# Rotary embedding with scaled positions on one core: rows of 16 KB, fp32 stores from SyncE, and a copy inside DRAM ahead of the positions

## The chip, the core and the metric

The kernel runs on one core of a Trainium2 chip. A core has five engines that run their own instruction streams: TensorE (PE in the profile, with PEld for its weight loads), VectorE (DVE), ScalarE (ACT), GpSimd (POOL) and SyncE (SP). SP, ScalarE and POOL also issue DMA transfers, which 16 DMA engines carry out. Each issuer has a queue of its own on each of them. The metric is the device time of one execution in microseconds (us), as a median over runs. The profile shows one execution.

## The reference

Input x has the shape (8, 8, 1024, 64) in fp32. Position and frequency give an angle, and each row of 64 values is turned by it, the first half against the second:

```python
    half = x.shape[-1] // 2
    scaled_positions = positions * scale
    angles = np.outer(scaled_positions, freqs)
    cos = np.cos(angles)
    sin = np.sin(angles)
    ...
    out_first = x_first * cos - x_second * sin
    out_second = x_first * sin + x_second * cos
    return np.concatenate([out_first, out_second], axis=-1).astype(np.float32)
```

Here scale is 0.5, positions run from 0 to 1023, and there are 32 frequencies. Input and output are 16.8 MB each. Sine and cosine depend on position and frequency alone and are the same for all 64 heads.

## The kernel before

The 64 heads are cut into 16 units of four heads (1 MiB of fp32 each). In a unit each of the 128 partitions holds 32 consecutive positions of one head: a row of 2048 values, 8 KB in DRAM (lines 42 to 46). Because 32 partitions make one head, partition p holds the same positions in every unit, and one table of sines and one of cosines (128 x 1024, fp16) serve all of them.

Loads: unit 0 is loaded in fp32 by SP (line 63). The other fifteen are loaded by POOL in seven DMAs of one to three units, cast to fp16 on the way (lines 76 to 81, `GROUPS`). ScalarE's queue brings the positions, four DMAs that each fill 32 partitions with the same 1024 positions (lines 67 to 71), and then the frequencies (line 73).

Setup: TensorE multiplies a row of constants with the frequencies, which spreads them, scaled, over all partitions in PSUM (`cfreq`, line 87). VectorE casts the positions (`posf`, line 90) and forms the angle in turns (`y`, line 95). The helper `reduced` takes off whole turns with the rounding constant `_MAGIC` in two instructions (lines 107 and 109); it runs once for the sine and, after a quarter turn is added (line 115), once for the cosine. ScalarE evaluates `Sin` for both (lines 117 and 119).

Main loop (lines 124 to 138), for each unit: two products of the whole unit, `pc` with the cosine and `ps` with the sine, then a subtraction and an addition over one half each, written into the fp16 tile `OUT`. All four run on VectorE. POOL stores `OUT` with a cast to fp32 (line 138). There are three buffers each for `pc` and `ps` and ten for `OUT`. The inputs have a buffer for every unit, so no load waits for a free one.

Order: a scheduler places the instructions and their waits from what each reads and writes. Each engine runs its own stream in order, and each queue takes its DMAs in the order of issue. POOL's stores therefore stand behind POOL's loads.

Of the kernel before, what the change touches and what calls it, by code (L numbers as in the profile page):

```python
# [1 line left out]

# [1 line left out]

# [4 lines left out]

FP32 = mybir.dt.float32
FP16 = mybir.dt.float16
I32 = mybir.dt.int32
AF = mybir.ActivationFunctionType
ALU = mybir.AluOpType

_MAGIC = 12582912.0
_TWO_PI_DN = float(np.float32(np.uint32(0x40C90FDA).view(np.float32)))


GROUPS = (1, 1, 2, 2, 3, 3, 3)
BUF_O = 10
BUF_P = 3


@with_exitstack
def kernel(
    ctx: ExitStack,
    tc: tile.TileContext,
    x: bass.AP,  # L30
    freqs: bass.AP,
    positions: bass.AP,
    scale: bass.AP,
    out: bass.AP,
):
    nc = tc.nc

    B, Hh, S, D = x.shape
    NBH = B * Hh
    half = D // 2  # L40
    P = nc.NUM_PARTITIONS
    HEADS = 4
    HP = P // HEADS
    K = S // HP
    N = K * D
    NU = NBH // HEADS
    assert S % HP == 0 and D == 2 * half and NBH % HEADS == 0 and sum(GROUPS) == NU - 1

    fscale = float(scale)

    xv = x.rearrange("b h s d -> (b h s d)").rearrange("(u p n) -> p u n", p=P, n=N)
    ov = out.rearrange("b h s d -> (b h s d)").rearrange("(u p n) -> p u n", p=P, n=N)

    consts = ctx.enter_context(tc.tile_pool(name="consts", bufs=1))
    tmp = ctx.enter_context(tc.tile_pool(name="tmp", bufs=1))
    setup_psum = ctx.enter_context(tc.tile_pool(name="setup_psum", bufs=1, space=bass.MemoryType.PSUM))
    xin = ctx.enter_context(tc.tile_pool(name="xin", bufs=1))
    xout = ctx.enter_context(tc.tile_pool(name="xout", bufs=BUF_O))
    prods = ctx.enter_context(tc.tile_pool(name="prods", bufs=BUF_P))


    X0 = xin.tile([P, N], FP32, name="X0")
    nc.sync.dma_start(out=X0, in_=xv[:, 0, :])
    xtiles = {0: X0}

    pos_i64 = consts.tile([P, K], positions.dtype)
    for h in range(HEADS):
        nc.scalar.dma_start(  # L68
            out=pos_i64[h * HP : (h + 1) * HP, :],
            in_=positions.rearrange("(q k) -> q k", k=K),  # L70
        )
    freq_row = consts.tile([1, half], FP32)
    nc.scalar.dma_start(out=freq_row, in_=freqs[None, :])

    u0 = 1
    for g, n in enumerate(GROUPS):
        X = xin.tile([P, n, N], FP16, name=f"X{g + 1}")
        nc.gpsimd.dma_start(out=X, in_=xv[:, u0 : u0 + n, :])  # L78
        for i in range(n):
            xtiles[u0 + i] = X[:, i, :]  # L80
        u0 += n


    coef = consts.tile([1, P], FP32)
    nc.vector.memset(coef, fscale / (2.0 * np.pi))  # L85
    cfreq = setup_psum.tile([P, half], FP32)
    nc.tensor.matmul(out=cfreq, lhsT=coef, rhs=freq_row, start=True, stop=True)  # L87

    posf = consts.tile([P, K], FP32)
    nc.vector.tensor_copy(  # L90
        out=posf,
        in_=pos_i64.bitcast(I32).rearrange("p (k t) -> p k t", t=2)[:, :, 0],
    )
    y = tmp.tile([P, K, half], FP32)
    nc.vector.tensor_tensor(  # L95
        out=y,
        in0=posf.unsqueeze(2).broadcast_to((P, K, half)),
        in1=cfreq.unsqueeze(1).broadcast_to((P, K, half)),
        op=ALU.mult,
    )  # L100

    cosT = consts.tile([P, K, half], FP16)
    sinT = consts.tile([P, K, half], FP16)

    def reduced(src, tag):
        m = tmp.tile([P, K, half], FP32, name="m" + tag)
        nc.vector.tensor_scalar(out=m, in0=src, scalar1=_MAGIC, scalar2=None, op0=ALU.add)  # L107
        rneg = tmp.tile([P, K, half], FP32, name="rneg" + tag)
        nc.vector.scalar_tensor_tensor(  # L109
            out=rneg, in0=m, scalar=_MAGIC, in1=src, op0=ALU.subtract, op1=ALU.subtract  # L110
        )
        return rneg

    yc = tmp.tile([P, K, half], FP32)
    nc.vector.tensor_scalar(out=yc, in0=y, scalar1=0.25, scalar2=None, op0=ALU.add)  # L115
    rc = reduced(yc, "c")
    nc.scalar.activation(out=cosT, in_=rc, func=AF.Sin, bias=0.0, scale=-_TWO_PI_DN)  # L117
    rs = reduced(y, "s")
    nc.scalar.activation(out=sinT, in_=rs, func=AF.Sin, bias=0.0, scale=-_TWO_PI_DN)  # L119
    cos_b = cosT.unsqueeze(2).broadcast_to((P, K, 2, half))  # L120
    sin_b = sinT.unsqueeze(2).broadcast_to((P, K, 2, half))


    for u in range(NU):
        X = xtiles.pop(u).rearrange("p (k h j) -> p k h j", h=2, j=half)
        pc = prods.tile([P, K, 2, half], FP16, tag="pc")
        ps = prods.tile([P, K, 2, half], FP16, tag="ps")
        nc.vector.tensor_tensor(out=pc, in0=X, in1=cos_b, op=ALU.mult)  # L128
        nc.vector.tensor_tensor(out=ps, in0=X, in1=sin_b, op=ALU.mult)  # L129

        OUT = xout.tile([P, K, 2, half], FP16, tag="O")
        nc.vector.tensor_tensor(  # L132
            out=OUT[:, :, 0, :], in0=pc[:, :, 0, :], in1=ps[:, :, 1, :], op=ALU.subtract
        )
        nc.vector.tensor_tensor(  # L135
            out=OUT[:, :, 1, :], in0=ps[:, :, 0, :], in1=pc[:, :, 1, :], op=ALU.add
        )
        nc.gpsimd.dma_start(out=ov[:, u, :], in_=OUT.rearrange("p k h j -> p (k h j)"))  # L138


# [1 line left out]
_INS = ['x', 'freqs', 'positions', 'scale']  # L142
_OUTS = [((8, 8, 1024, 64), 'float32')]

_NUMBERS = {'scale': 0.5}


# [26 lines left out]
```

## Time and profile before

| | |
|---|---|
| median of 10 runs | 85.99 us (85.86 to 86.16) |
| the profiled execution | 86.14 us, its span 84.4 us |
| busy: VectorE / POOL / ScalarE / TensorE | 63.6 / 13.7 / 3.4 / 0.6 us |
| share of the span taken by packets of POOL's DMA queue (16 engines) | 98.9% |
| bytes read from and written to HBM | 16.81 MB and 16.78 MB |
| y, the first work on both positions and frequencies, starts | 9.18 us |
| last VectorE instruction starts / last store is issued | 71.85 / 72.83 us |

The span runs from the first to the last instruction that the profile holds; the device time lies about 1.7 us above it. In rows of groups, "128x2048 f16" is partitions x elements per partition and type, "x15" the count; after the bar come the busy time, the mean of one in ns, and the idle time of the engine before them with what ended it. In the slices a digit is the busy share in tenths. A DMA row names the issuing queue, the size, and the median time from issue to landing. Queue q0 is POOL's, q1 SP's, q10 ScalarE's. The window rows give, for a stretch, each engine's busy time, the clock, the share of the DMA engines' time and the GB/s that they wrote.

### The profile page before, as it was taken

How to read it: one execution, taken by the hardware profiler on the slowest of the kernel's cores; microseconds unless marked ns; L12 is line 12 of the kernel's file. 1: busy time of each engine (PE TensorE's matmuls, PEld its weight loads, DVE VectorE, ACT ScalarE, POOL GpSimd, SP SyncE). 2: the span in 40 equal slices, each digit the busy share in tenths (PEclk: the TensorE clock that was granted, in tenths of full speed). 3: DMA queues.
4: the chain of work that ended last, by engine and by line, in shares of the span. 5: the costliest groups of instructions: out<-in, count | busy, mean ns of one | idle time of the engine just before them, and what ended most of it. 6: DMA issues, size and time to landing. Idle time of an engine off the chain costs nothing.

```text
span 84.4 us, 183 instructions
## 1 busy us (share of the span) xinstructions
PE 0.6 (1%) x2; PEld 0.5 (1%) x2; DVE 63.6 (75%) x72; ACT 3.4 (4%) x3; POOL 13.7 (16%) x27
## 2 busy tenths in 40 slices
PE   0000200000000000000000000000000000000000
PEld 0000200000000000000000000000000000000000
DVE  0000699999999999999999999999999999300000
ACT  0410005400000000000000000000000000000000
POOL 5980000000202202112021020220202202200000
DMA  1899999999999999999999999999999999999970
GB/s 16 338 284 206 216 216 216 216 218 210 216 212 210 218 216 216 216 216 218 165 418 423 435 420 427 420 431 431 431 431 420 435 420 423 431 431 423 435 284 0
DMA packets 4675, 25.73 MB, mean 305 GB/s; under 512 B 578, under 2 KB 578, under 8 KB 2498
## 3 DMA queue, kind: packets, MB, share of 16 engines
q0 software_dynamic: 4336, 24.64, 98.9%
q1 hardware_dynamic: 144, 1.05, 3.3%
q10 hardware_dynamic: 194, 0.03, 0.3%
q14 instruction: 1, 0.01, 0.0%
HBM read 16.81 MB, written 16.78 MB: 398 GB/s over the span
## 4 chain that ended last, share of the span: by engine, by line
DVE 38%; issue 32%; DMA 7%; POOL 6%; ACTq 2%; POOLq 1%; PE 1%
DVE pc L128 12%; DVE ps L129 11%; DMA freq_row<-in_freqs_dram 7%; POOL out_dram L138 6%; DVE OUT L135 5%; DVE OUT L132 5%; ACTq L68 2%; DVE y L95 1%; DVE rnegc L109 1%; DVE yc L115 1%; PE cfreq L87 1%; DVE ms L107 1%; DVE mc L107 1%; POOLq L169 1%; POOLq L138 0%
## 5 line engine op out<-in xcount | busy, mean ns | idle before, releaser
L129 DVE TENSOR_TENSOR ps<-X,sinT 128x2048 f16<-128x2048 f16 (+1 forms) x16 | 20.5, 1282 | 0.0
L128 DVE TENSOR_TENSOR pc<-X,cosT 128x2048 f16<-128x2048 f16 (+1 forms) x16 | 20.4, 1281 | 0.0
L138 POOL DMA_DIRECT2D out_dram<-OUT x16 | 8.6, 538 | 58.6 <-DVE OUT L135 58.6
L132 DVE TENSOR_TENSOR OUT<-pc,ps 128x1024 f16<-128x1024 f16 x16 | 10.9, 682 | 0.0
L135 DVE TENSOR_TENSOR OUT<-ps,pc 128x1024 f16<-128x1024 f16 x16 | 10.9, 681 | 0.0
L90 DVE CAST posf<-pos_i 128x32 f32<-128x32 int32 x1 | 0.2, 181 | 7.1 <-DMA pos_i<-in_positions_dram 7.1
L78 POOL DMA_DIRECT2D X<-in_x_dram x7 | 4.9, 714 | 0.8 <-POOLq L155 0.8
L95 DVE TENSOR_TENSOR y<-posf,cfreq 128x1024 f32<-128x1024 f32 x1 | 1.2, 1222 | 0.9 <-PE cfreq L87 0.9
L119 ACT ACTIVATE sinT<-rnegs 128x1024 f16<-128x1024 f32 x1 | 1.1, 1057 | 9.0 <-DVE rnegs L109 9.0
L119 ACT ACT_TABLE_LOAD x1 | 1.3, 1283 | 3.2 <-issue 3.2
L109 DVE SCALAR_TENSOR_TENSOR rnegc<-mc,yc 128x1024 f32<-128x1024 f32 x1 | 1.2, 1217 | 0.0
L109 DVE SCALAR_TENSOR_TENSOR rnegs<-ms,y 128x1024 f32<-128x1024 f32 x1 | 1.2, 1215 | 0.0
L117 ACT ACTIVATE cosT<-rnegc 128x1024 f16<-128x1024 f32 x1 | 1.1, 1057 | 0.1
L85 DVE MEMSET coef<- 1x128 f32 x1 | 0.2, 165 | 0.8 <-PEq L155 0.8
L115 DVE TENSOR_SCALAR yc<-y 128x1024 f32<-128x1024 f32 x1 | 0.7, 693 | 0.0
L107 DVE TENSOR_SCALAR ms<-y 128x1024 f32<-128x1024 f32 x1 | 0.7, 686 | 0.0
L107 DVE TENSOR_SCALAR mc<-yc 128x1024 f32<-128x1024 f32 x1 | 0.7, 685 | 0.0
L87 PE MATMUL cfreq<-freq_row,coef 1*128 1x32 f32 x2 | 0.6, 392 | 8.5 <-DMA freq_row<-in_freqs_dram 8.5
L87 PEld LDWEIGHTS cfreq<-freq_row,coef 1*128 1x128 f32 x2 | 0.5, 306 | 8.5 <-DVE posf L90 8.5
L155 POOL MEMSET const-float32-0.0<- 128x1 f32 x1 | 0.1, 99 | 0.2 <-issue 0.2
L155 POOL MEMSET const-bfloat16-1.0<- 128x1 bf16 x1 | 0.1, 102 | 0.0
L155 POOL MEMSET const-uint8-127<- 128x1 uint8 x1 | 0.1, 100 | 0.0
(1 smaller groups left out, 0.1 us busy)
## 6 DMA issues: line engine op xcount, KB each, us to landing
out_dram<-OUT POOLq DMA_DIRECT2D x16, 1024.0 KB, 16.6
X<-in_x_dram POOLq DMA_DIRECT2D x3, 1536.0 KB, 30.7
X<-in_x_dram POOLq DMA_DIRECT2D x2, 1024.0 KB, 15.4
X<-in_x_dram SPq DMA_DIRECT2D x1, 1024.0 KB, 5.1
X<-in_x_dram POOLq DMA_DIRECT2D x2, 512.0 KB, 8.0
pos_i<-in_positions_dram ACTq DMA_DIRECT2D x4, 8.0 KB, 5.0
freq_row<-in_freqs_dram ACTq DMA_DIRECT2D x1, 0.1 KB
```

The lines of the kernel that those rows point to most:

```text
L68: nc.scalar.dma_start(out=pos_i64[h * HP : (h + 1) * HP, :], in_=positions.rearrange("(q k) -> q k", k=K),)
L78: nc.gpsimd.dma_start(out=X, in_=xv[:, u0 : u0 + n, :])
L87: nc.tensor.matmul(out=cfreq, lhsT=coef, rhs=freq_row, start=True, stop=True)
L95: nc.vector.tensor_tensor(out=y, in0=posf.unsqueeze(2).broadcast_to((P, K, half)), in1=cfreq.unsqueeze(1).broadcast_to((P, K, half)), op=A ...
L107: nc.vector.tensor_scalar(out=m, in0=src, scalar1=_MAGIC, scalar2=None, op0=ALU.add)
L109: nc.vector.scalar_tensor_tensor(out=rneg, in0=m, scalar=_MAGIC, in1=src, op0=ALU.subtract, op1=ALU.subtract)
L119: nc.scalar.activation(out=sinT, in_=rs, func=AF.Sin, bias=0.0, scale=-_TWO_PI_DN)
L128: nc.vector.tensor_tensor(out=pc, in0=X, in1=cos_b, op=ALU.mult)
L129: nc.vector.tensor_tensor(out=ps, in0=X, in1=sin_b, op=ALU.mult)
L132: nc.vector.tensor_tensor(out=OUT[:, :, 0, :], in0=pc[:, :, 0, :], in1=ps[:, :, 1, :], op=ALU.subtract)
L135: nc.vector.tensor_tensor(out=OUT[:, :, 1, :], in0=ps[:, :, 0, :], in1=pc[:, :, 1, :], op=ALU.add)
L138: nc.gpsimd.dma_start(out=ov[:, u, :], in_=OUT.rearrange("p k h j -> p (k h j)"))
```

## The change

A unit is now eight heads, 2 MiB: each partition holds 64 positions, a row of 4096 values, 16 KB in DRAM. There are 8 units. Unit 0 still comes in fp32 from SP, and ScalarE casts it into an fp16 tile. Units 1 to 7 come from POOL, one DMA each, cast to fp16. The loop takes unit 1 before unit 0. In the loop only `ps` has a tile of its own; the cosine product, the subtraction and the addition are written into the input tile. ScalarE then copies the result to an fp32 tile (four buffers), and SP stores that.

The first DMA on ScalarE's queue is new: it copies 16 rows of 512 bytes from x to out inside DRAM, two to each unit's part of out. The unit stores later write over them. Positions are loaded once, onto 16 partitions, and a matmul with a 0/1 matrix `sel`, which POOL builds, spreads them over 128. The range reduction runs once; the cosine comes from the absolute value of the reduced angle (sign bit masked off) and a bias of a quarter turn. `pin` keeps instructions of an engine in the order in which they are written.

```diff
--- before.py
+++ after.py
@@ -17,10 +17,8 @@
 _MAGIC = 12582912.0
 _TWO_PI_DN = float(np.float32(np.uint32(0x40C90FDA).view(np.float32)))
 
-
-GROUPS = (1, 1, 2, 2, 3, 3, 3)
-BUF_O = 10
-BUF_P = 3
+BUF_O = 4
+BUF_P = 2
 
 
 @with_exitstack
@@ -39,103 +37,118 @@
     NBH = B * Hh
     half = D // 2
     P = nc.NUM_PARTITIONS
-    HEADS = 4
+    HEADS = 8
     HP = P // HEADS
     K = S // HP
     N = K * D
     NU = NBH // HEADS
-    assert S % HP == 0 and D == 2 * half and NBH % HEADS == 0 and sum(GROUPS) == NU - 1
+    assert S % HP == 0 and D == 2 * half and NBH % HEADS == 0
 
     fscale = float(scale)
 
-    xv = x.rearrange("b h s d -> (b h s d)").rearrange("(u p n) -> p u n", p=P, n=N)
-    ov = out.rearrange("b h s d -> (b h s d)").rearrange("(u p n) -> p u n", p=P, n=N)
+    xv = x.rearrange("b h s d -> (b h s d)").rearrange("(u p n) -> u p n", p=P, n=N)
+    ov = out.rearrange("b h s d -> (b h s d)").rearrange("(u p n) -> u p n", p=P, n=N)
 
     consts = ctx.enter_context(tc.tile_pool(name="consts", bufs=1))
     tmp = ctx.enter_context(tc.tile_pool(name="tmp", bufs=1))
-    setup_psum = ctx.enter_context(tc.tile_pool(name="setup_psum", bufs=1, space=bass.MemoryType.PSUM))
+    psum = ctx.enter_context(tc.tile_pool(name="psum", bufs=1, space=bass.MemoryType.PSUM))
     xin = ctx.enter_context(tc.tile_pool(name="xin", bufs=1))
     xout = ctx.enter_context(tc.tile_pool(name="xout", bufs=BUF_O))
     prods = ctx.enter_context(tc.tile_pool(name="prods", bufs=BUF_P))
 
 
-    X0 = xin.tile([P, N], FP32, name="X0")
-    nc.sync.dma_start(out=X0, in_=xv[:, 0, :])
-    xtiles = {0: X0}
+    X0f = xin.tile([P, N], FP32, name="X0f")
+    nc.sync.dma_start(out=X0f, in_=xv[0])
 
-    pos_i64 = consts.tile([P, K], positions.dtype)
-    for h in range(HEADS):
-        nc.scalar.dma_start(
-            out=pos_i64[h * HP : (h + 1) * HP, :],
-            in_=positions.rearrange("(q k) -> q k", k=K),
-        )
+
+    R = 16
+    xr = x.rearrange("b h s d -> (b h s d)").rearrange("(r n) -> r n", r=R)
+    outr = out.rearrange("b h s d -> (b h s d)").rearrange("(r n) -> r n", r=R)
+    nc.scalar.dma_start(out=outr[:, 0:128], in_=xr[:, 0:128])
+
+    pos_i64 = consts.tile([HP, K], positions.dtype)
+    nc.scalar.dma_start(out=pos_i64, in_=positions.rearrange("(q k) -> q k", k=K))
     freq_row = consts.tile([1, half], FP32)
     nc.scalar.dma_start(out=freq_row, in_=freqs[None, :])
 
-    u0 = 1
-    for g, n in enumerate(GROUPS):
-        X = xin.tile([P, n, N], FP16, name=f"X{g + 1}")
-        nc.gpsimd.dma_start(out=X, in_=xv[:, u0 : u0 + n, :])
-        for i in range(n):
-            xtiles[u0 + i] = X[:, i, :]
-        u0 += n
+    X = [xin.tile([P, K, 2, half], FP16, name=f"X{u}") for u in range(NU)]
+
+    def load(u):
+        nc.gpsimd.dma_start(out=X[u].rearrange("p k h j -> p (k h j)"), in_=xv[u])
+
+
+    sel = consts.tile([HP, HEADS, HP], FP32)
+    load(1)
+    nc.gpsimd.memset(sel, 0.0)
+    nc.gpsimd.affine_select(
+        out=sel, in_=sel, compare_op=ALU.not_equal, fill=1.0, base=0,
+        pattern=[[0, HEADS], [-1, HP]], channel_multiplier=1,
+    )
+    for u in range(2, NU):
+        load(u)
+
+    pin = tc.keep_in_program_order
 
 
     coef = consts.tile([1, P], FP32)
-    nc.vector.memset(coef, fscale / (2.0 * np.pi))
-    cfreq = setup_psum.tile([P, half], FP32)
+    pin(nc.vector.memset(coef, fscale / (2.0 * np.pi)))
+    quarter = consts.tile([P, 1], FP32)
+    pin(nc.vector.memset(quarter, np.pi / 2.0))
+    cfreq = psum.tile([P, half], FP32)
     nc.tensor.matmul(out=cfreq, lhsT=coef, rhs=freq_row, start=True, stop=True)
 
+    pos_row = consts.tile([HP, K], FP32)
+    pin(nc.vector.tensor_copy(
+        out=pos_row,
+        in_=pos_i64.bitcast(I32).rearrange("p (k t) -> p k t", t=2)[:, :, 0],
+    ))
+    pos_ps = psum.tile([P, K], FP32)
+    nc.tensor.matmul(
+        out=pos_ps, lhsT=sel.rearrange("q a b -> q (a b)"), rhs=pos_row, start=True, stop=True
+    )
     posf = consts.tile([P, K], FP32)
-    nc.vector.tensor_copy(
-        out=posf,
-        in_=pos_i64.bitcast(I32).rearrange("p (k t) -> p k t", t=2)[:, :, 0],
-    )
+    pin(nc.vector.tensor_copy(out=posf, in_=pos_ps))
+
     y = tmp.tile([P, K, half], FP32)
-    nc.vector.tensor_tensor(
+    pin(nc.vector.tensor_tensor(
         out=y,
         in0=posf.unsqueeze(2).broadcast_to((P, K, half)),
         in1=cfreq.unsqueeze(1).broadcast_to((P, K, half)),
         op=ALU.mult,
-    )
+    ))
+    m = tmp.tile([P, K, half], FP32)
+    pin(nc.vector.tensor_scalar(out=m, in0=y, scalar1=_MAGIC, scalar2=None, op0=ALU.add))
+    r = tmp.tile([P, K, half], FP32)
+    pin(nc.vector.scalar_tensor_tensor(
+        out=r, in0=m, scalar=_MAGIC, in1=y, op0=ALU.subtract, op1=ALU.subtract
+    ))
+    sinT = consts.tile([P, K, half], FP16)
+    pin(nc.scalar.activation(out=sinT, in_=r, func=AF.Sin, bias=0.0, scale=-_TWO_PI_DN))
+    ra = tmp.tile([P, K, half], FP32)
+    pin(nc.vector.tensor_scalar(
+        out=ra.bitcast(I32), in0=r.bitcast(I32), scalar1=0x7FFFFFFF, scalar2=None, op0=ALU.bitwise_and
+    ))
+    cosT = consts.tile([P, K, half], FP16)
+    pin(nc.scalar.activation(out=cosT, in_=ra, func=AF.Sin, bias=quarter, scale=-_TWO_PI_DN))
+    pin(nc.scalar.copy(out=X[0].rearrange("p k h j -> p (k h j)"), in_=X0f))
 
-    cosT = consts.tile([P, K, half], FP16)
-    sinT = consts.tile([P, K, half], FP16)
-
-    def reduced(src, tag):
-        m = tmp.tile([P, K, half], FP32, name="m" + tag)
-        nc.vector.tensor_scalar(out=m, in0=src, scalar1=_MAGIC, scalar2=None, op0=ALU.add)
-        rneg = tmp.tile([P, K, half], FP32, name="rneg" + tag)
-        nc.vector.scalar_tensor_tensor(
-            out=rneg, in0=m, scalar=_MAGIC, in1=src, op0=ALU.subtract, op1=ALU.subtract
-        )
-        return rneg
-
-    yc = tmp.tile([P, K, half], FP32)
-    nc.vector.tensor_scalar(out=yc, in0=y, scalar1=0.25, scalar2=None, op0=ALU.add)
-    rc = reduced(yc, "c")
-    nc.scalar.activation(out=cosT, in_=rc, func=AF.Sin, bias=0.0, scale=-_TWO_PI_DN)
-    rs = reduced(y, "s")
-    nc.scalar.activation(out=sinT, in_=rs, func=AF.Sin, bias=0.0, scale=-_TWO_PI_DN)
     cos_b = cosT.unsqueeze(2).broadcast_to((P, K, 2, half))
     sin_b = sinT.unsqueeze(2).broadcast_to((P, K, 2, half))
 
 
-    for u in range(NU):
-        X = xtiles.pop(u).rearrange("p (k h j) -> p k h j", h=2, j=half)
-        pc = prods.tile([P, K, 2, half], FP16, tag="pc")
+    for u in (1, 0, *range(2, NU)):
         ps = prods.tile([P, K, 2, half], FP16, tag="ps")
-        nc.vector.tensor_tensor(out=pc, in0=X, in1=cos_b, op=ALU.mult)
-        nc.vector.tensor_tensor(out=ps, in0=X, in1=sin_b, op=ALU.mult)
-
-        OUT = xout.tile([P, K, 2, half], FP16, tag="O")
-        nc.vector.tensor_tensor(
-            out=OUT[:, :, 0, :], in0=pc[:, :, 0, :], in1=ps[:, :, 1, :], op=ALU.subtract
-        )
-        nc.vector.tensor_tensor(
-            out=OUT[:, :, 1, :], in0=ps[:, :, 0, :], in1=pc[:, :, 1, :], op=ALU.add
-        )
-        nc.gpsimd.dma_start(out=ov[:, u, :], in_=OUT.rearrange("p k h j -> p (k h j)"))
+        pin(nc.vector.tensor_tensor(out=ps, in0=X[u], in1=sin_b, op=ALU.mult))
+        pin(nc.vector.tensor_tensor(out=X[u], in0=X[u], in1=cos_b, op=ALU.mult))
+        pin(nc.vector.tensor_tensor(
+            out=X[u][:, :, 0, :], in0=X[u][:, :, 0, :], in1=ps[:, :, 1, :], op=ALU.subtract
+        ))
+        pin(nc.vector.tensor_tensor(
+            out=X[u][:, :, 1, :], in0=ps[:, :, 0, :], in1=X[u][:, :, 1, :], op=ALU.add
+        ))
+        OUT = xout.tile([P, N], FP32, tag="O")
+        pin(nc.scalar.copy(out=OUT, in_=X[u].rearrange("p k h j -> p (k h j)")))
+        nc.sync.dma_start(out=ov[u], in_=OUT)
 
 
 # ---- launch: one core; inputs and outputs as the reference has them ----
```

## The prediction

> **What bounds the kernel now.** I read the page first, then windows, then the DMA queues of the first microseconds, then the costliest groups. The page (40 slices; GB/s counts bytes as written):
>
> ```profile
> span 84.4 us, 183 instructions
> ...
> DVE  0000699999999999999999999999999999300000
> ...
> DMA  1899999999999999999999999999999999999970
> GB/s 16 338 284 206 216 216 216 216 218 210 216 212 210 218 216 216 216 216 218 165 418 423 435 420 427 420 431 431 431 431 420 435 420 423 431 431 423 435 284 0
> ```
>
> VectorE ends near 72.5 us, the DMA engines work until about 82. So transfers set the end. Windows (length, each engine's busy time, clock, DMA share, GB/s) show two phases:
>
> ```profile
> 10.00:40.00 30.00, 0.00 (x0) 0.00 (x0) 29.97 (x33) 2.11 (x2) 3.29 (x6) 1.00 1.07 215
> 40.00:42.50 2.50, 0.00 (x0) 0.00 (x0) 2.50 (x4) 0.00 (x0) 0.00 (x0) 1.00 0.97 185
> 44.00:79.00 35.00, 0.00 (x0) 0.00 (x0) 28.50 (x34) 0.00 (x0) 4.80 (x9) 1.00 1.12 427
> ```
>
> Loads come first, because the stores stand behind them in POOL's queue. 215 GB/s written in fp16 is 430 read in fp32; the stores write 427. Either way about 428 GB/s of fp32, and the 33.59 MB that HBM read and wrote (16.81 + 16.78) take 78.5 us at that rate.
>
> The setup is the other chain. Three windows of the DMA queues, 2.50 to 3.95, 3.95 to 4.85 and 4.85 to 5.55 us (packets, MB, share; q1 is SP's X0, q10 ScalarE's positions and frequencies, q0 POOL's):
>
> ```profile
> q10 hardware_dynamic: 48, 0.01, 3.1%
> ...
> q1 hardware_dynamic: 46, 0.38, 102.3%
> ...
> q0 software_dynamic: 25, 0.10, 73.1%
> q1 hardware_dynamic: 23, 0.06, 21.5%
> q10 hardware_dynamic: 53, 0.01, 7.8%
> ```
>
> 48 packets are one position DMA (32 data, 16 completions). The first got in between X0's packets; the second, issued at 1.17 us, moved nothing until X0 ran out, and then went at once, as did q0. What ScalarE issues second waits for all of X0. Critical chain (start, duration) and groups:
>
> ```profile
> 2.58 5.83 DMA freq_row<-in_freqs_dram
> 8.54 0.62 PE cfreq L87 x2
> 9.18 1.23 DVE y L95
> ```
> ```profile
> L129 DVE TENSOR_TENSOR ps<-X,sinT 128x2048 f16<-128x2048 f16 x15 | 18.2, 1215 | 0.0
> L132 DVE TENSOR_TENSOR OUT<-pc,ps 128x1024 f16<-128x1024 f16 x16 | 10.9, 682 | 0.0
> L119 ACT ACTIVATE sinT<-rnegs 128x1024 f16<-128x1024 f32 x1 | 1.1, 1057 | 9.0 <-DVE rnegs L109 9.0
> ...
> X<-in_x_dram SPq DMA_DIRECT2D x1, 1024.0 KB, 5.1
> ```
>
> **What the Trainium skill says.** "VectorE: DVE Perf Modes", The perf-mode tier table: a 16-bit tensor-tensor of 2048 elements takes 1224 ns; the trace has 1215, and in-place operands keep type and stride, so I keep that rate. "DMA: Bandwidth & Descriptors", Queues, rings and completion order: each DMA engine takes turns between queues by packet. The trace agrees once q0 runs, but not from 3.95 to 4.85; the measurement decides. Same page, Latency and other measured facts: copies of 128 x 16 KiB tiles between HBM tensors reach 214 GB/s per direction, 428 together; no run here yet shows mixed traffic, so this is why I assume no loss from it.
>
> **The change part by part.**
>
> *Bytes and stores.* The fp32 bytes stay. A floor: SP's X0 took 5.10 us from issue (0.74) to landing, 2.45 of it for 1.05 MB at 428, so 2.65 us is start, ramp and completion. 0.74 + 2.65 + 78.5 = 81.9 if the engines never idle. The last store now lands at 72.83 + 9.8 = 82.6, leaving 1.8 us to the span's end. Floor: 83.7, against 84.4; the gain is the dip at 40 to 42.5 us and ragged ends.
>
> *Setup, ScalarE's queue.* Three position DMAs go (0.44 us of issue each); a copy inside DRAM comes first, at 0.74. It takes the place of the first position DMA, the one that got in. Positions become second, frequencies third. X0f is twice X0: the q1 packets that ended between 4.9 and 5.5 us end at 7.3 to 8.0 (+2.45). Then positions land at about 8.3. Frequencies need a data and a completion packet, each behind one of q0's (0.33 us now, perhaps double with longer rows): landing about 9.3, against 8.41. The wait holds TensorE, then VectorE's y, and everything after it.
>
> *Positions spread by a matmul.* From frequencies to y took 0.77 us (8.41 to 9.18). A second matmul and a copy out of PSUM come between, unless TensorE does the positions first: 0 to 0.9, I take 0.5. y starts at 10.6. POOL builds the selector after its first load; no row shows its cost, but it has until 8.3 us, and X1's 4.9 us of transfer covers the delay of the later loads. Nothing.
>
> *Tables.* 2048 elements instead of 1024. y and the subtraction 2.29 each (the fp32 form of L129 took 2293 ns); the rounding add 0.69 + 0.53 = 1.22; sine 1.057 + 1024 x 0.833 = 1.91, with the element rate of "ScalarE: Activation LUTs", What ACT_TABLE_LOAD costs (its 186 ns + 0.833 per element gives 1039 where the trace has 1057). With four hand-overs of 0.04: sine ready at 10.6 + 7.71 + 0.15 = 18.45. The mask runs on VectorE beside the sine. If it doesn't get the faster rate it takes 2.2 us instead of 1.2 and costs 0.35. The cosine ends at 20.4, when the second product wants it (20.65).
>
> *Main loop.* Steps were 1.137 us for 2048 elements and 0.603 for 1024, so 1024 more cost 0.534. A unit of twice the size: 2 x 2.205 + 2 x 1.137 = 6.68; eight, 53.5; VectorE ends at 71.95. The first unit's two fp32 products go (2.15 us saved on VectorE). Their cast moves to ScalarE, 1.057 + 3072 x 0.833 = 3.62 us, from 20.4 to 24.0, a microsecond before unit 0 is wanted (25.1); a second table load (1.28) would cost 0.3. The output cast, also 3.62, runs beside the next unit, except the last: 75.6. Four output buffers suffice: the first must be free 26.7 us after it is filled. The stores' wait for the DRAM copy is over long before the first of them (28.8). SP has nothing else queued behind them.
>
> *Sum.* The last store, alone on the engines, takes 5.10 + 2.45 = 7.55 from issue: lands at 83.15, span 84.95. That is above the floor of 83.7, so the end moves from transfers to VectorE's chain. The profiled execution took 86.14, its span plus 1.74, and lay 0.15 above the median; 84.95 + 1.59 = 86.5, or 0.6% slower.
>
> **The rivals.** *Small loads get in (faster).* If the engines' turns include positions and frequencies before X0f is finished, y starts at about 9.0, the chain ends at 83.35, below the floor, and the floor gives 83.7 + 1.6 = 85.3. For it: the first position DMA did get in. Against: the window 3.95 to 4.85. It decides below y = 9.35; the chain equals today's span at y = 10.05. *Stores crowd out loads.* The first store starts near 29.8 us with 12 us of loads left. At equal shares the last lands near 54, wanted at 65.2. If a 16 KB store packet alternates with an 8 KB load packet, loads get a third and end at 65.8: 1.2 us late, 87.7. Above that share it grows; if stores always went first, loads would keep 27% and be 9 us late. Against: loads are seven units early. *Plain fp32 stores are slower.* X0, the only plain transfer, ran at 419 GB/s from 3.95 to 4.85. Stores at 410 would add 1.7 us to the floor: 87.0. *The DRAM copy blocks its queue.* If its completion in DRAM holds positions 1.5 us beyond X0f: 88.0; no row shows such a transfer, the bound below is zero, since X0f covers it.
>
> **How the numbers follow.** My chain 0.42 (its own range 85.8 to 87.2), small loads get in 0.22, slower stores 0.15, crowding 0.13, blocked queue 0.08. About 0.2% is what measurements of this kernel can tell from no change: below 85.82 lie the second case nearly whole and a little of the first, 0.24; within, 0.08; above, 0.68. The range 85.1 to 88.9 leaves out the bottom of the second case and the tails of crowding and blocking.
>
> **What would show it.** q10 idle between the DRAM copy and X0f's end; frequencies landing near 9.3; y at 10.6; products of 2.28 us; 6.68 us per unit without gaps; ScalarE's cast of 3.62; the chain of waits ending through VectorE, ScalarE and one store of about 7.5 us. Wrong if y starts before 10, if VectorE waits for a load, or if the DMA engines stay full up to the last landing.

## The result and the profile after

The changed kernel takes 88.9 us (88.37 to 89.19, 9 runs) against 85.99: slower by a factor of 1.0336 (95% interval 1.0321 to 1.0351). The direction was forecast and the time lies at the upper edge of the range, but the size was not: 2.9 us instead of 0.5. The profiled execution has a span of 87.3 us where 84.95 was forecast.

The page of the changed kernel, the same rows as before:

```profile
span 87.3 us, 153 instructions
...
DVE  0000029996999999999999999999999999900000
...
DMA  5799999999999999999999998999999882990991
GB/s 105 255 349 323 263 214 221 206 233 203 218 218 203 233 203 203 289 282 390 297 304 323 360 458 383 473 413 428 458 390 465 375 360 120 435 405 0 480 413 68
```

VectorE now ends at 76.2 us, and near the end the DMA engines have gaps: one slice moves nothing. Three windows over the last 18 us (length, busy time of each engine, clock, DMA share, GB/s) show that they wait for stores:

```profile
69.00:75.00 6.00, 0.00 (x0) 0.00 (x0) 5.93 (x5) 3.60 (x1) 0.00 (x0) 1.00 0.62 265
75.00:81.00 6.00, 0.00 (x0) 0.00 (x0) 1.20 (x2) 3.61 (x1) 0.00 (x0) 1.00 0.72 306
81.00:87.30 6.30, 0.00 (x0) 0.00 (x0) 0.00 (x0) 0.00 (x0) 0.00 (x0) 1.00 0.69 291
```

The end has moved from the bytes to VectorE's chain, as forecast. The chain that ended last (start, duration) says where it begins:

```profile
2.02 9.28 DMA freq_row<-in_freqs_dram
...
11.44 0.60 PE cfreq L98 x2
12.04 0.49 PE pos_ps L106 x2
...
12.56 0.24 DVE posf L110
...
12.82 2.30 DVE y L113
```

Frequencies land at 11.30 us instead of 8.41 before, and y starts at 12.82 instead of 9.18. The DMA queues (packets, MB, share) from 1.7 to 5.5 us, and from 5.5 to 8.0 us, show the reason:

```profile
q1 hardware_dynamic: 77, 1.26, 103.1%
...
q0 software_dynamic: 32, 0.26, 50.0%
q1 hardware_dynamic: 32, 0.52, 50.0%
q10 hardware_dynamic: 32, 0.01, 1.4%
```

Until 5.5 us only X0f (q1) moves. Then the three queues take strict turns, 32 packets each, two per DMA engine in 2.5 us. So one small packet of ScalarE's queue (q10) costs a turn of about 1.23 us: one 16 KB packet of q1, 611 ns at the median, and one of POOL's loads, 624 ns. The copy has two of them ahead of the positions on every engine, its row and its completion.

The second part of the loss is in the loop. One unit in order of time:

```profile
62.28 2.28 DVE L141 TENSOR_TENSOR ps<-X,sinT 128x4096 f16<-128x4096 f16 x1
...
64.60 2.29 DVE L142 TENSOR_TENSOR X<-X,cosT 128x4096 f16<-128x4096 f16 x1
66.92 1.22 DVE L143 TENSOR_TENSOR X<-X,ps 128x2048 f16<-128x2048 f16 x1
68.07 1.22 DVE L146 TENSOR_TENSOR X<-ps,X 128x2048 f16<-128x2048 f16 x1
69.20 2.28 DVE L141 TENSOR_TENSOR ps<-X,sinT 128x4096 f16<-128x4096 f16 x1
```

From unit to unit it takes 69.20 - 62.28 = 6.92 us; 6.68 was forecast. The products take the forecast 2.28 each, but L142 starts 2.32 us after L141 and L143 2.32 after L142, where 2.205 was assumed. Both wait on the instruction just ahead of them: L142 writes X in place, which L141 has to have read, and L143 reads what L142 wrote. L146 starts 1.15 after L143, as an instruction does that waits for none on VectorE. In the kernel before, the order was another. The start of its loop in the chain, and a later unit in order of time:

```profile
14.61 2.28 DVE ps L129
16.88 3.33 DVE pc L128 x2
20.22 0.60 DVE OUT L132
...
56.09 1.22 DVE L129 TENSOR_TENSOR ps<-X,sinT 128x2048 f16<-128x2048 f16 x1
57.23 1.21 DVE L128 TENSOR_TENSOR pc<-X,cosT 128x2048 f16<-128x2048 f16 x1
58.36 0.68 DVE L132 TENSOR_TENSOR OUT<-pc,ps 128x1024 f16<-128x1024 f16 x1
58.97 0.68 DVE L135 TENSOR_TENSOR OUT<-ps,pc 128x1024 f16<-128x1024 f16 x1
```

Two cosine products (`pc`) ran ahead of the first subtraction (L132), so the scheduler had put the next unit's cosine product between `ps` and the subtraction. The `ps` that is waited for had ended at 57.31, 1.05 us before the subtraction started.

### The profile page after: what moved, and what is told of

It is laid out like the page before. It is cut to its first block, busy times and chain, and to the rows that moved or that the text cites. A ratio compares the mean times of both kernels' runs of the same rounds, so it can differ in the third digit from the quotient of the medians.

```text
span 87.3 us, 153 instructions
## 1 busy us (share of the span) xinstructions
PE 1.1 (1%) x4; PEld 0.9 (1%) x4; DVE 62.5 (72%) x40; ACT 37.4 (43%) x12; POOL 4.5 (5%) x13
## 4 chain that ended last, share of the span: by engine, by line
DVE 69%; DMA 11%; ACT 6%; ACTq 1%; DVEq 1%; PE 1%; issue 1%
DVE X L142 21%; DVE ps L141 20%; DVE X L143 11%; DMA freq_row<-in_freqs_dram 11%; DVE X L146 9%; ACT OUT L150 4%; DVE r L122 3%; DVE y L113 3%; ACT sinT L126 2%; DVE m L120 1%; DVEq L182 1%; ACTq L70 1%; ACTq L67 1%; PE cfreq L98 1%; PE pos_ps L106 1%
## 5 line engine op out<-in xcount | busy, mean ns | idle before, releaser
L150 ACT CAST OUT<-X 128x4096 f32<-128x4096 f16 x8 | 28.8, 3606 | 25.0 <-DVE X L146 25.0
L141 DVE TENSOR_TENSOR ps<-X,sinT 128x4096 f16<-128x4096 f16 x8 | 18.3, 2284 | 0.7 <-ACT sinT L126 0.7
L142 DVE TENSOR_TENSOR X<-X,cosT 128x4096 f16<-128x4096 f16 x8 | 18.3, 2292 | 0.3
L143 DVE TENSOR_TENSOR X<-X,ps 128x2048 f16<-128x2048 f16 x8 | 9.8, 1224 | 0.3
L146 DVE TENSOR_TENSOR X<-ps,X 128x2048 f16<-128x2048 f16 x8 | 9.7, 1218 | 0.0
L126 ACT ACTIVATE sinT<-r 128x2048 f16<-128x2048 f32 x1 | 1.9, 1910 | 14.7 <-DVE r L122 14.7
L133 ACT CAST X<-X0f 128x4096 f16<-128x4096 f32 x1 | 3.6, 3589 | 0.0
L122 DVE SCALAR_TENSOR_TENSOR r<-m,y 128x2048 f32<-128x2048 f32 x1 | 2.3, 2293 | 0.0
L113 DVE TENSOR_TENSOR y<-posf,cfreq 128x2048 f32<-128x2048 f32 x1 | 2.3, 2287 | 0.0
L132 ACT ACTIVATE cosT<-ra,quarter 128x2048 f16<-128x2048 f32 x1 | 2.0, 1987 | 0.0
```

What stands on the lines that cost most here:

```text
L113: pin(nc.vector.tensor_tensor(out=y, in0=posf.unsqueeze(2).broadcast_to((P, K, half)), in1=cfreq.unsqueeze(1).broadcast_to((P, K, half)), ...
L122: pin(nc.vector.scalar_tensor_tensor(out=r, in0=m, scalar=_MAGIC, in1=y, op0=ALU.subtract, op1=ALU.subtract))
L126: pin(nc.scalar.activation(out=sinT, in_=r, func=AF.Sin, bias=0.0, scale=-_TWO_PI_DN))
L133: pin(nc.scalar.copy(out=X[0].rearrange("p k h j -> p (k h j)"), in_=X0f))
L141: pin(nc.vector.tensor_tensor(out=ps, in0=X[u], in1=sin_b, op=ALU.mult))
L142: pin(nc.vector.tensor_tensor(out=X[u], in0=X[u], in1=cos_b, op=ALU.mult))
```

## The experiments

Eight kernels, each a small edit of the changed kernel. Ratios are against the kernel before.

### Without the copy

```diff
-    nc.scalar.dma_start(out=outr[:, 0:128], in_=xr[:, 0:128])
```

> The changed kernel without the copy inside DRAM; positions and frequencies are then first and second on ScalarE's queue. Theory A (every small packet waits for one 16 KB packet of X0f and one of POOL's load, 1.23 us, and the copy owns two packets per engine ahead of the positions): frequencies land at 11.30 - 2 x 1.23 = 8.84 us, y starts near 10.4 instead of 12.82, the span falls by 2.4 to 84.9, about 86.5 us. Rival B (the small loads simply wait until X0f is through, whatever stands ahead of them): frequencies land within 0.6 us of 11.30 and the time stays above 88.2. Rival C (the end is set by the bytes from now on): y moves by 2.4 but the time by less than 1.2.

Measured: 85.5 us, ratio 0.9953 (0.9935 to 0.997). The chain of this kernel:

```profile
1.18 6.67 DMA freq_row<-in_freqs_dram
...
9.36 2.30 DVE y L112
```

and its queues from 1.7 to 4.5 us, then from 4.5 to 5.6:

```profile
q1 hardware_dynamic: 49, 0.80, 96.8%
q10 hardware_dynamic: 32, 0.01, 2.9%
...
q1 hardware_dynamic: 28, 0.46, 98.6%
```

y starts 3.46 us earlier and the time falls by 3.4: rivals B and C are out. Without the copy the whole loss is gone, and what is left of the change is 0.5% faster than the kernel before. The longer steps of the loop are still there; with so early a y they are hidden, because the DMA engines are full (share 1.01 from 69 to 75 us, 0.94 from 75 to 81). The copy costs more than theory A's two turns, though. Without it the positions, now the first request, get in between X0f's packets before 4.5 us (32 packets: 16 rows and 16 completions). The frequencies, the second, wait until 5.6. In the changed kernel not even the first request, the copy, got in.

### The same rows, written to SBUF

```diff
-    nc.scalar.dma_start(out=outr[:, 0:128], in_=xr[:, 0:128])
+    scratch = consts.tile([R, 128], FP32)
+    nc.scalar.dma_start(out=scratch, in_=xr[:, 0:128])
```

> The same sixteen rows of 512 bytes are read at the same place of ScalarE's queue, but written to an SBUF tile that nothing reads, instead of to out. Theory A (turns of packets): nothing changes, frequencies land at 11.3, 88.9 us. Rival D (a copy inside DRAM completes late and blocks what stands behind it): frequencies land 1 to 2.5 us earlier and the time falls to 86.5 to 88.

Measured: 87.65 us, ratio 1.0201 (1.0184 to 1.0219). Its chain:

```profile
1.65 8.16 DMA freq_row<-in_freqs_dram
...
11.32 2.30 DVE y L114
```

and its queues from 1.7 to 4.5 us:

```profile
q1 hardware_dynamic: 50, 0.82, 97.3%
q10 hardware_dynamic: 32, 0.01, 1.7%
```

Theory A isn't enough: the destination matters. D's numbers fit, its mechanism doesn't, since in the changed kernel the copy itself doesn't move before 5.5 us. So the cost has two parts. A request standing first, whatever it writes, takes 1.96 us (y from 9.36 to 11.32): it uses up the place that gets in. A destination in DRAM takes 1.50 more (to 12.82): the place is lost. ScalarE needs 0.60 us to issue the copy to DRAM and 0.41 for the one to SBUF, so it may only be late. That is theory H, tried below.

### X0f in shorter rows

```diff
-    nc.sync.dma_start(out=X0f, in_=xv[0])
+    for c in range(2):
+        nc.sync.dma_start(out=X0f[:, c * (N // 2) : (c + 1) * (N // 2)], in_=xv[0][:, c * (N // 2) : (c + 1) * (N // 2)])
```

> The copy stays; X0f is loaded by two DMAs of 8 KB rows instead of one of 16 KB rows, the same bytes. Theory A (a turn lasts as long as the packets of the other queues): a turn shrinks from 0.61 + 0.62 to 0.31 + 0.62 us; five turns before the frequencies' packet save 1.5 us, more if the packets accepted ahead of the small ones are shorter too: frequencies at 8 to 9.8, 85.6 to 87.4 us. Rival B (they wait for X0f's bytes): frequencies at 11.3 or later, 88.9 or more.

Measured: 87.01 us, ratio 1.0116 (1.0081 to 1.0151); the profiled execution, at 86.32, was one of the quicker ones. Chain, and the queues from 4.8 to 7.3 us:

```profile
2.02 6.54 DMA freq_row<-in_freqs_dram
...
10.08 2.30 DVE y L114
```
```profile
q0 software_dynamic: 35, 0.29, 54.6%
q1 hardware_dynamic: 77, 0.51, 49.6%
q10 hardware_dynamic: 59, 0.02, 3.0%
```

Frequencies land at 8.56 instead of 11.30, inside theory A's 8 to 9.8. In 2.5 us q10 moves 59 packets; in the changed kernel it moved 32. POOL's queue (q0) sets in last, at 5.2 us. From 5.3 to 7.3 us all three take turns:

```profile
q0 software_dynamic: 33, 0.27, 64.3%
q1 hardware_dynamic: 42, 0.32, 38.9%
q10 hardware_dynamic: 35, 0.01, 2.0%
```

35 packets on 16 engines in 2.0 us make a turn of 0.91 us; theory A has 0.31 + 0.62 = 0.93. Rival B is out again: X0f's bytes are the same. Once the small packets take part, they wait for the length of the others' packets, not for X0f's end. The edit also makes two transfers of one, and q10 moves from 4.8 us on instead of 5.5. Which of the two brought that forward, the shorter rows or the earlier end of the first transfer, this run doesn't tell.

### Frequencies on SP's queue ahead of X0f

```diff
-    nc.scalar.dma_start(out=freq_row, in_=freqs[None, :])
...
+    nc.sync.dma_start(out=freq_row, in_=freqs[None, :])
     nc.sync.dma_start(out=X0f, in_=xv[0])
```

> The copy stays first on ScalarE's queue; the frequencies move to SP's queue ahead of X0f, which so starts 0.4 us later. Theory H (a small request gets in only if it is issued before the engines have taken in X0f's rows; the copy, with 0.60 us of issue instead of 0.41, comes too late): the copy's packets now move at 2.8 to 4 us instead of 5.5, the positions' at about 6, y at 8.5 to 9.5, 85.2 to 86.2 us. Rival D2 (a copy inside DRAM waits for X0f whenever it is issued): the copy's packets at 5.5 or later, the positions' at 8.0 or later, y at 10.3 to 11.5, 86.5 to 87.5 us.

Measured: 85.95 us, ratio 0.9982 (0.9961 to 1.0004). The queues from 1.6 to 2.5 us, then from 2.5 to 5.9:

```profile
q1 hardware_dynamic: 13, 0.18, 107.1%
q10 hardware_dynamic: 32, 0.01, 3.8%
...
q1 hardware_dynamic: 65, 1.06, 79.5%
```

With X0f issued at 1.13 instead of 0.75 us, all 32 packets of the copy moved before 2.5 us, earlier than the 2.8 to 4 that H expected: ahead of X0f and not between its packets. Then q10 is silent, and the positions, second, start at 5.95. y starts at 9.72, a little after the 8.5 to 9.5 expected; the time lies inside H's range and below D2's. So D2 is out: a copy inside DRAM doesn't always wait for X0f, and 0.38 us more of a head start were enough here. That in the changed kernel the 0.19 us decide by which its issue is longer than that of the copy to SBUF fits all runs, but no run changes them alone.

### The copy last

```diff
-    nc.scalar.dma_start(out=outr[:, 0:128], in_=xr[:, 0:128])
...
     nc.scalar.dma_start(out=freq_row, in_=freqs[None, :])
+    nc.scalar.dma_start(out=outr[:, 0:128], in_=xr[:, 0:128])
```

> The copy inside DRAM is issued last on ScalarE's queue, after the frequencies, instead of first. Theory A2 (what the copy costs is its place ahead of the positions and frequencies, nothing else): as without the copy, frequencies at 7.85, y at 9.4, 85.5 us. Rival G (the copy itself, or the wait of the first store on it, costs time wherever it stands): 86.2 or more.

Measured: 85.39 us, ratio 0.9927 (0.9904 to 0.9951); y starts at 9.07. The copy costs nothing where it stands behind the small loads: rival G is out. The kernel is faster than both, before and changed; from the run without the copy (85.5) four executions hardly tell it apart.

### VectorE's order alone

The sine product of the next unit goes ahead of the subtraction and addition of the last one (`finish` holds these two, ScalarE's cast and the store):

```diff
+    late = None
     for u in (1, 0, *range(2, NU)):
         ps = prods.tile([P, K, 2, half], FP16, tag="ps")
         pin(nc.vector.tensor_tensor(out=ps, in0=X[u], in1=sin_b, op=ALU.mult))
+        if late is not None:
+            finish(*late)
         pin(nc.vector.tensor_tensor(out=X[u], in0=X[u], in1=cos_b, op=ALU.mult))
+        late = (u, ps)
+    finish(*late)
```

> The copy stays. VectorE's order alone: the subtraction and addition of a unit come after the next unit's sine product and before its cosine product, all still in place. Theory E (the step of 6.92 us per unit instead of 6.68 is two waits on an instruction that ended just before, 0.1 us each[...]): 6.68 us per unit, VectorE ends 1.6 us earlier, the time falls by 1.2 to 1.7 to 87.2 to 87.7. Rival F (in-place operands, or ScalarE's casts beside them, slow VectorE): still 6.9 per unit, 88.9 us.

Measured: 88.6 us, ratio 1.0293 (1.0257 to 1.0329): a gain of 0.3 us, neither theory's number. The profiled execution, at 87.99, was the quickest of four (the others 88.59 to 88.64), and its y starts at 12.08 already. So only what follows the sine is compared here. The waits of this kernel have a new line (waited for, in total, times, longest):

```profile
DVE ps L153 <- ACT X L133: 0.7, 1, 0.7
```

VectorE now reaches unit 0 before ScalarE has cast it and waits 0.7 us. From the sine's end to VectorE's end this kernel took 54.6 us (19.90 to 74.54) against 55.6 (20.64 to 76.22). The next run takes the stall away.

```diff
-    for u in (1, 0, *range(2, NU)):
+    for u in (1, 2, 0, *range(3, NU)):
```

> As the reorder run (copy kept, VectorE's order changed), but unit 0, which waits for ScalarE's cast, is taken third instead of second. Theory E (the in-place waits cost 0.24 us per unit, and the first reorder run lost the gain to a stall of VectorE on that cast): no stall, VectorE's last instruction ends 1.7 us earlier than the changed kernel's for the same start of y, 87.0 to 87.5 us. Rival F: the step per unit is still 6.9 and the time 88.6 or more.

Measured: 87.63 us, ratio 1.0181 (1.0149 to 1.0213). Two starts of the cosine product and what lies between:

```profile
56.35 2.28 DVE L156 TENSOR_TENSOR X<-X,cosT 128x4096 f16<-128x4096 f16 x1
...
58.55 2.28 DVE L153 TENSOR_TENSOR ps<-X,sinT 128x4096 f16<-128x4096 f16 x1
60.76 1.21 DVE L140 TENSOR_TENSOR X<-X,ps 128x2048 f16<-128x2048 f16 x1
61.89 1.21 DVE L143 TENSOR_TENSOR X<-ps,X 128x2048 f16<-128x2048 f16 x1
63.03 2.28 DVE L156 TENSOR_TENSOR X<-X,cosT 128x4096 f16<-128x4096 f16 x1
```

63.03 - 56.35 = 6.68 us per unit, with the same in-place operands and the same casts on ScalarE beside them. From y's start to VectorE's end it is 61.66 us instead of 63.40: 1.74 earlier, of which the time shows 1.27, so that it lies 0.13 above theory E's range. Part of the difference lies outside the profile. In the three kernels with the new order the device time is 2.03 to 2.06 us above the span (medians), in the changed kernel and the other five 1.76 to 1.81. What these 0.27 us are, no run shows. Rival F is out. The 0.24 us per unit come from the two waits on an instruction that has only just ended.

### All of it together

No copy, positions first on ScalarE's queue, frequencies on SP's ahead of X0f, and the order of the last run.

```diff
-    nc.scalar.dma_start(out=outr[:, 0:128], in_=xr[:, 0:128])
-    nc.scalar.dma_start(out=freq_row, in_=freqs[None, :])
...
+    nc.sync.dma_start(out=freq_row, in_=freqs[None, :])
     nc.sync.dma_start(out=X0f, in_=xv[0])
...
-    for u in (1, 0, *range(2, NU)):
+    for u in (1, 2, 0, *range(3, NU)):
```

> No copy, positions first on ScalarE's queue, frequencies on SP's ahead of X0f, and the order of reorder_x0_third. Theory: both small loads get in, frequencies land by 4.5, y starts near 5.5, VectorE's chain ends 5 us or more before it would set the end, and the bytes set it: packets end near 82, 84.6 to 85.4 us. Rival I (the end follows VectorE's chain all the way down): 82 us or less.

Measured: 85.89 us, ratio 0.9988 (0.9976 to 1.0). Its timeline and its window from 70 to 82 us:

```profile
4.02 2.29 DVE L112 TENSOR_TENSOR y<-posf,cfreq 128x2048 f32<-128x2048 f32 x1
```
```profile
70.00:82.00 12.00, 0.00 (x0) 0.00 (x0) 0.00 (x0) 1.85 (x1) 0.00 (x0) 1.00 0.97 416
```

y starts 8.8 us earlier than in the changed kernel and VectorE ends at 68.2, but the DMA engines are full to 82. Rival I is out; the bytes set the end. One product even waits 3.0 us for its load. The time is 0.5 above the range expected, and no better than the kernel before. The span of 83.8 is the floor of the forecast (83.7). The run with the copy last, with y at 9.07 and a span of 83.6, already stands at that floor. Of the 0.5 us by which it is quicker than this one (85.39 against 85.89), about half are the 0.27 outside the span; the rest is open.

## Why the prediction was wrong

The main mechanism was right: VectorE's chain, held up by the frequencies, passes the bytes and sets the end. That the change would be slower was partly luck: the forecast hung on 0.5 us, and four of its terms were off by more, two each way. The terms of the span add up as follows (us):

| term | forecast | measured |
|---|---|---|
| frequencies land | 9.3 | 11.30 |
| to the start of y | 1.3 | 1.52 |
| y to the sine | 7.85 | 7.85 |
| eight units | 53.5 | 55.55 |
| last cast, with its hand-over | 3.65 | 3.67 |
| last store, issue to landing | 7.55 | 6.3 |
| landing to the span's end | 1.8 | 1.1 |
| sum | 84.95 | 87.29 |

*ScalarE's queue* is the step that failed first, by 2.0 us. Two of its statements were wrong. "It takes the place of the first position DMA, the one that got in": the copy got in nowhere. With SBUF as its destination it did get in, and y came 1.50 us earlier; with X0f issued 0.38 us later it moved before X0f. Being late fits both, but isn't shown alone. "What ScalarE issues second waits for all of X0", carried over to X0f, named the wrong end. In the kernel before, the silence ended when nearly all of X0 had moved (121 of its 128 packets by 4.85 us). With X0f twice as long it ended near 5.5 us, with 77 of 128 packets moved, earlier than the 7.3 to 8.0 I took. Then about five turns followed, of some 1.23 us while X0f lasted, where I had counted the frequencies' two at 0.33 or double. The early end of the silence and the long turns went opposite ways and left a net 2.0.

*Main loop*, by 2.05: the steps of 1.137 and 0.603 came from an order in which nothing waited on its direct predecessor. I carried them to an order in which two of four do. The reordered run gives 6.68 back.

*The last store* went the other way by 1.25, and the stretch after it by 0.7: X0's 5.10 us from issue to landing, of which 2.65 were not transfer, were too much for a late store, where 6.3 - 4.9 = 1.4 were not (why, no run tells), and the 1.8 us behind a store of POOL's are 1.1 behind one of SP's.

Confirmed were y to the sine, to the hundredth; both casts; four output buffers and the stores' wait on the copy at nothing; and the floor. The rival in which small loads get in came true in part, and only in kernels where the copy isn't ahead of them: there the positions got in and the frequencies didn't, and the time went to the floor (85.5 without the copy; 85.3 forecast). One sum among the rivals was off: loads that end at 65.8 and are wanted at 65.2 are 0.6 us late, not 1.2. It decided nothing. Slower plain stores and crowding didn't appear: no product waits for a load in the changed kernel's list of waits, and from 69 to 75 us the kernel without the copy moves 431 GB/s, all of it stores.

## What to carry to other kernels

Count what a small transfer stands behind in turns of packets: here each packet ahead of it in its own queue cost one packet of every other busy queue, 1.23 us with 16 KB rows and 0.91 where one of the two other queues had 8 KB rows. Issue what opens the compute chain first, ahead of large loads and of anything that isn't needed soon. A step time taken from a trace holds only for the order in which it was taken: look at what each instruction waits for, and put another instruction between a producer and its reader.

## What the runs showed of the hardware

- A request issued on ScalarE's queue at 0.74 us, together with SP's X0f, got in between X0f's first packets where its issue took 0.41 us (positions, copy to SBUF); where it took 0.60 (copy inside DRAM) it didn't. Issued 0.38 us ahead of X0f, the copy moved before it. A request issued at 1.18 us or later waited until 5.5 us or later in every run with X0f in one transfer, though X0f still had packets left. POOL's queue starts then too (in the changed kernel no packet before 5.5 us). What sets this time stays open. With rows of 16 KB it ended after some five packets of each engine (77 of 128). With rows of 8 KB it ended after about seven, near 4.8 us: 112 packets with X0f in two transfers, 121 of 128 in the kernel before. There the transfer in front was also nearly through.
- A copy inside DRAM takes ScalarE 0.60 us to issue, and the small load behind it 0.61 (positions); after a copy to SBUF (0.41) it takes 0.44.
- On VectorE, a product of 4096 elements is followed after 2.32 us by an instruction that waits for it, and after 2.20 by one that doesn't.
